# Substitution coefficients of the delta rule: fifteen shuffles within VectorE in place of a way through memory

## The chip, the cores and the metric

One Trainium2 chip, one core. The metric is the device time of one execution in microseconds (us). TensorE (PE) multiplies matrices, VectorE (DVE) and ScalarE (ACT) work on 128 partitions of elements, GpSimd (POOL) on few things here, and SyncE (SP) issues the DMA transfers. Each engine runs its own queue in order; semaphores join them.

## What is computed

A trunk of two layers over 256 positions and a width of 1024, in float32. A layer is a half-step SwiGLU network, a mixer, and a second such network. The mixer projects its input into three branches and their gates: A (sparse attention with an indexer that picks 64 keys per query), B (attention with forget gates) and C (gated DeltaNet). The change lies in C:

```python
def chunked_gated_delta_rule(q, k, v, g, beta):
    ...
    a_mat = jnp.where(strict, jnp.einsum('nbhid,nbhjd->nbhij', kb, kc) * decay, 0.0)
    m = a_mat + jnp.eye(cs, dtype=jnp.float32)
    rhs = jnp.concatenate([vc * bc[..., None], kb * jnp.exp(gc)[..., None]], axis=-1)
    sol = lax.linalg.triangular_solve(m, rhs, left_side=True, lower=True, unit_diagonal=True)
    ...
    y_c = rms_norm(o_c, delta_norm) * jax.nn.silu(c_z.reshape(b, s, C_HEADS, C_HEAD_DIM))
```

followed by `merged = gates[0] * y_a + gates[1] * y_b + gates[2] * y_c`, each y times a branch matrix of its own, and an output projection.

## The kernel before

All weights are streamed: SP issues `raw` tiles of 128 x 2 x 512 (line 121), ACT copies each to a rounded `hi`, DVE subtracts for the rest `lo` (lines 135 and 136), and PE multiplies with both. A weight unit has a number; in layer 0 the mixer has the units 48 to 127: 80 to 83 are `bv`, 84 to 91 the gates of branch A, 92 to 99 those of B, 100 to 103 branch A's matrix, 104 to 111 the gates of C, 112 to 115 branch B's matrix, 116 to 119 branch C's, 120 to 127 the output's. Three `hi` and `lo` are held at a time, so a `hi` waits until PE is through with the unit three before it.

The branches are generators (`branch_a`, `branch_b`, `branch_c`), which the class Emit steps along between the large matmuls by a plan of its own (`tick`, line 178): a step is due when the time that the plan gives to its engines has gone by, and no step is written while the planned DVE or ACT is over 6 us ahead of PE (`LIM`). `finish` (line 185) writes what is left of a branch before its matrix is used. A scheduler then orders the written instructions on each engine; the large tiles of one kind (`k4`, 20 of them) are handed out in the order of writing.

Branch C computes 8 triangular systems of 128 x 128 (two halves of the positions, four heads) by inverting their 16 x 16 diagonal blocks on DVE and merging the blocks upward on PE. `nT` holds the transposed matrix; `nd` its diagonal blocks, `cp16` (line 629) these packed to 128 x 128: partition 16k + i has, for each of the 8 systems, row i of block k. The substitution (lines 669 to 673) is, for m = 0 to 14, one product `ztmp<-nb,zc` and one difference `zc<-zc,ztmp`. Its coefficients `nb` must hold row m of a block in all 16 partitions of this block; they come through memory: `dr<-cp16` (line 632) writes 128 x 128 to DRAM, two transfers `nb<-dr` (line 634) read them back 16 times repeated, all three on SP's queue.

From `zc` come Z (the block inverse) and X, its transpose (lines 678 to 682). Then on PE, with a copy or a sum on ACT or DVE behind each: `lw` (blocks of 16 to 32), `lv` twice (32 to 64), `xz` (a transpose), `lv` twice (64 to 128), `vh` (the solve), `st` (state), `wv`, `ks`, `qs`, `vh` and `wv` for the second half of the positions, and `yc`. The last matmuls of the mixer's middle, `pbr` with `ych`, need them all.

Other names: `qs<-tq` and `ix` belong to branch A's queries and index scores, `score` and MAX/MATCH_REPLACE to its choice of keys, `lg` are logits in PSUM, `L` logits in SBUF and then softmax, `mx` their maximum, `pT`/`PT` transposed softmax, `pv`/`yh`/`yl` its product with the values, `bqk` and `bv` branch B's inputs, `gate` the copy of a gate's matmul out of PSUM.

Of the kernel before, what the change touches and what calls it, by code (L numbers as in the profile page):

```python
# [9 lines left out]
F32 = mybir.dt.float32  # L10
# [6 lines left out]
P = 128  # L17
# [177 lines left out]
def trunk_kernel(ctx: ExitStack, tc: tile.TileContext, x, consts, par, rows, bgate, fnorm,  # L195
                 wf1i, wf1o, wf2i, wf2o, wmx, wms, wbr, wmo, out, phases=None):
    nc = tc.nc
# [3 lines left out]
    rawp = ctx.enter_context(tc.tile_pool(name="rawp", bufs=NR))  # L201
    hlp = ctx.enter_context(tc.tile_pool(name="hlp", bufs=NH))
    wk = ctx.enter_context(tc.tile_pool(name="wk", bufs=2))
    dp = ctx.enter_context(tc.tile_pool(name="dp", bufs=2, space=bass.MemoryType.DRAM))
    ps = ctx.enter_context(tc.tile_pool(name="ps", bufs=4, space=bass.MemoryType.PSUM))
    pa = ctx.enter_context(tc.tile_pool(name="pa", bufs=2, space=bass.MemoryType.PSUM))
    pc = ctx.enter_context(tc.tile_pool(name="pc", bufs=2, space=bass.MemoryType.PSUM))
# [19 lines left out]
    V, S, G = E.V, E.S, E.G  # L227
# [11 lines left out]
    for u in range(4):  # L239
# [6 lines left out]
                                   ap=[[0, P], [N_ROW, DEPTH], [1, N_ROW]]))  # L246
# [12 lines left out]
    def k4(name, dt=F32):  # L259
        return wk.tile([P, 1024], dt, name=name, tag="k4", bufs=K4)  # L260
# [20 lines left out]
    def v3(t, a):  # L281
        return t.rearrange("p (a b) -> p a b", a=a)
# [210 lines left out]
    def tiny(name, n, bufs=2):  # L493
        return wk.tile([P, n], F32, name=name, tag="t_" + name, bufs=bufs)
# [80 lines left out]
    def branch_c(l, qkv, gd, hh, hl, need):  # L575
# [48 lines left out]
        nd, nb, zc = k4("nd"), [k4("nb") for _ in range(2)], tiny("zc", P, 1)  # L624
# [3 lines left out]
        cp16 = tiny("cp16", P, 1)  # L628
        V.tensor_reduce(v3(cp16, 8), nd.rearrange("p (q k r) -> p q r k", q=8, k=8), axis=AX.X, op=OP.add)
        V.tensor_copy(v3(zc, 8), cst[:, None, C_E16:C_E16 + 16].to_broadcast([P, 8, 16]))  # L630
        dr = dp.tile([P, P], F32, name="dr", tag="dr")
        nc.sync.dma_start(dr, cp16)
        for i in range(2):
            nc.sync.dma_start(nb[i], bass.AP(tensor=dr.tensor, offset=dr.offset + i * 1024,
                                               ap=[[2048, 8], [0, 16], [1, 1024]]))
        yield
        rk = tiny("rk", 8)
        G.tensor_tensor(out=rk, in0=ssk, in1=phalf, op=OP.pow)
        kdf = tiny("kdf", 4)
# [28 lines left out]
        tmp = tiny("ztmp", P, 1)  # L668
        for m in range(15):
            k = 15 - m  # L670
            V.tensor_tensor(out=v3(tmp, 8)[:, :, :k], in0=nb[m // 8].rearrange("p (m q r) -> p m q r", m=8, q=8)[:, m % 8, :, m + 1:],
                            in1=zv[:, :, m:m + 1].to_broadcast([P, 8, k]), op=OP.mult)
            V.tensor_tensor(out=zv[:, :, m + 1:], in0=zv[:, :, m + 1:], in1=v3(tmp, 8)[:, :, :k], op=OP.subtract)
            if m % 4 == 3:
                yield
# [325 lines left out]
    def mixer(pi, st):  # L1001
# [40 lines left out]
        with tc.high_priority(offset=EOFF):  # L1042
            for tb in range(2):
# [3 lines left out]
                S.activation(th, z, AF.Tanh, scale=0.5)  # L1047
                V.scalar_tensor_tensor(z, th, 1.0, z, op0=OP.add, op1=OP.mult)
        tcc = E.add(branch_c(l, qkv, gd, hh, hl, need), -1, CP)
        bqk = []  # L1050
        for i in range(2):
# [167 lines left out]
```

## Time and profile before

| | |
|---|---|
| runs | 1130.22 us median of 3 (1129.42 to 1130.91) |
| profiled execution | 1133.0 us, span 1131.2 us |
| PE busy | 1108.3 us, 98% |
| DVE busy | 842.2 us, 74% |
| ACT busy | 652.2 us, 58% |
| POOL busy | 198.0 us, 18% |

A busy PE is not PE at its peak, as matmuls overlap and their ends are modelled. What a change can win or lose is read from the places where PE stands, and from the granted clock of TensorE. The two mixers lie at 143 to 440 us and 700 to 1000 us; the second repeats the first.

### The profile page before, as it was taken

To read this page: it belongs to the slowest core of one execution; us is meant where nothing else is said; L and a number is where in the kernel's file an instruction comes from. 1 tells how busy PE (TensorE), PEld (TensorE's weight loads), DVE (VectorE), ACT (ScalarE), POOL (GpSimd) and SP (SyncE) were. 2 spreads that over 40 slices of the span, in tenths; PEclk is the share of its full clock that TensorE was granted. 3 is DMA by queue.
4 is the path that set the end of the run, shared out by engine and by line. 5 is a ranking of instruction groups with operands and counts; after the bars stand their busy time and mean duration, and the time that the engine had idled before them with its cause. 6 is when DMAs were issued, how large, how long until landed. Compare 5 with 4: busy or idle time off the path is not lost.

```text
span 1131.2 us, 17844 instructions
## 1 busy us (share of the span) xinstructions
PE 1108.3 (98%) x6765; PEld 954.2 (84%) x6765; DVE 842.2 (74%) x1373; ACT 652.2 (58%) x1136; POOL 198.0 (18%) x172
## 2 busy tenths in 40 slices
PE   9999999998999999999999999999999999999997
PEld 7888898987778878888888889979877788888886
DVE  7776689879746677876678767888796658787753
ACT  6655455644758645655465645564647685556543
POOL 4322022100000203322032311040000003033210
PEclk9999999999999999999999999999999999999999
DMA  8665655555434354666556555555554344556652
GB/s 285 205 186 189 190 178 184 165 146 167 149 113 144 128 179 154 213 195 188 187 171 202 186 193 182 177 169 168 152 177 150 104 130 147 169 171 200 187 191 91
DMA packets 56375, 194.07 MB, mean 172 GB/s; under 512 B 6240, under 2 KB 8672, under 8 KB 56288
## 3 DMA queue, kind: packets, MB, share of 16 engines
q1 hardware_dynamic: 55856, 192.32, 53.2%
q8 instruction: 53, 0.87, 0.3%
q10 hardware_dynamic: 432, 0.60, 0.1%
q14 instruction: 34, 0.28, 0.1%
HBM read 191.72 MB, written 1.18 MB: 171 GB/s over the span
## 4 chain that ended last, share of the span: by engine, by line
PE 91%; DVE 4%; DMA 2%; issue 1%; POOL 1%; ACT 1%; POOLq 0%; DVEq 0%; ACTq 0%
PE pw L148 48%; PE pt L148 25%; PE pbr L148 6%; PE po L148 4%; DMA nb<-dr 2%; DVE lo L86 1%; PE lg L148 1%; PE pv L148 1%; PE pT L152 1%; PE lv L148 1%; PE lw L148 1%; DVE score L86 1%; PE gq L148 1%; DVE ztmp L86 0%; POOL rp L86 0%
## 5 line engine op out<-in xcount | busy, mean ns | idle before, releaser
L86 DVE TENSOR_TENSOR lo<-raw,hi 128x1024 fp32r<-128x1024 f32 (+2 forms) x353 | 451.2, 1280 | 178.8 <-ACT hi L86 178.2
L86 ACT ACTIVATE hi<-raw 128x1024 fp32r<-128x1024 f32 (+2 forms) x353 | 372.6, 1057 | 353.9 <-PE pw L148 155.7
L148 PE MATMUL pw<-xt,hi 128*128 128x512 f32 x1024 | 349.0, 396 | 0.8 <-ACT hi L86 0.8
L148 PE MATMUL pw<-xt,lo 128*128 128x256 f32 x1024 | 263.8, 280 | 0.0
L148 PEld LDWEIGHTS pw<-xt,hi 128*128 128x128 f32 x1024 | 189.3, 189 | 37.7 <-ACT hi L86 1.7
L148 PE MATMUL pt<-hi,xt 128*128 128x512 f32 (+1 forms) x640 | 206.5, 398 | 4.7 <-DVE gate L86 4.7
L148 PEld LDWEIGHTS pw<-xt,lo 128*128 128x128 f32 x1024 | 193.0, 189 | 9.0 <-DVE lo L86 0.7
L148 PEld LDWEIGHTS pt<-hi,xt 128*128 128x128 f32 x640 | 120.5, 191 | 28.7 <-issue 5.8
L148 PE MATMUL pw<-ht,hi 128*128 128x512 f32 x384 | 132.2, 394 | 0.0
L148 PE MATMUL pt<-lo,xt 128*128 128x512 f32 (+1 forms) x320 | 127.9, 400 | 1.7 <-DVE lo L86 1.7
L148 PE MATMUL pt<-xt,hi 128*128 128x256 f32 x640 | 118.1, 285 | 0.0
L148 PE MATMUL pw<-ht,lo 128*128 128x256 f32 x384 | 103.4, 279 | 0.0
L148 PEld LDWEIGHTS pt<-xt,hi 128*128 128x128 f32 x640 | 99.6, 191 | 0.2
L148 PE MATMUL pt<-xt,lo 128*128 128x256 f32 x320 | 89.7, 284 | 0.0
L148 PEld LDWEIGHTS pw<-ht,hi 128*128 128x128 f32 x384 | 71.4, 188 | 15.2
L86 POOL TENSOR_TENSOR hr<-hg,rbc 128x512 f32<-128x512 f32 x32 | 42.3, 1323 | 213.8 <-DVE hg L86 204.5
L148 PEld LDWEIGHTS pw<-ht,lo 128*128 128x128 f32 x384 | 72.4, 188 | 1.5
L148 PEld LDWEIGHTS pt<-lo,xt 128*128 128x128 f32 x320 | 61.0, 191 | 14.2 <-DVE lo L86 2.6
L86 POOL TENSOR_TENSOR hg<-hr,rbc 128x512 f32<-128x512 f32 x32 | 66.9, 2090 | 2.5
L86 POOL TENSOR_TENSOR ssum<-ssum,sq 128x512 f32<-128x512 f32 x18 | 28.6, 1588 | 199.3 <-ACT sq L86 199.3
L148 PEld LDWEIGHTS pt<-xt,lo 128*128 128x128 f32 x320 | 60.8, 191 | 0.0
L86 POOL TENSOR_TENSOR so<-so,mhalf 128x8 f32<-128x8 f32 x2 | 3.3, 1642 | 284.9 <-DVE so L86 284.9
(254 smaller groups left out, 1498.6 us busy)
## 6 DMA issues: line engine op xcount, KB each, us to landing
raw<-in_wmx SPq DMA_DIRECT2D x112, 512.0 KB, 3.7
raw<-in_wf2i SPq DMA_DIRECT2D x64, 512.0 KB, 3.8
raw<-in_wf1i SPq DMA_DIRECT2D x63, 512.0 KB, 4.2
raw<-in_wf1o SPq DMA_DIRECT2D x32, 512.0 KB, 4.2
raw<-in_wf2o SPq DMA_DIRECT2D x32, 512.0 KB, 4.2
raw<-in_wbr SPq DMA_DIRECT2D x24, 512.0 KB, 3.3
raw<-in_wmo SPq DMA_DIRECT2D x16, 512.0 KB, 4.1
raw<-in_wms SPq DMA_DIRECT2D x8, 468.0 KB, 3.8
```

The lines of the kernel that those rows point to most:

```text
L86: return f(*args, **kw)
L148: self.nc.tensor.matmul(out, lhsT, rhs, start=start, stop=stop, skip_group_check=True)
L152: self.nc.tensor.transpose(out, in_, ident)
```

## The change

The DRAM tile and the three transfers go. In their place DVE writes `nb` itself: for each m one `stream_shuffle`, which gives every partition of a group of 32 the content of one partition out of this group, by a list of 32 places. The list for m sends partition m to partitions 0 to 15 and partition 16 + m to 16 to 31. Only the columns that the substitution reads are written, 8 x (15 - m). Where one `yield` stood behind the transfers, there are now three, one after each five shuffles. Nothing else is changed in the text.

```diff
-    dp = ctx.enter_context(tc.tile_pool(name="dp", bufs=2, space=bass.MemoryType.DRAM))
...
-        dr = dp.tile([P, P], F32, name="dr", tag="dr")
-        nc.sync.dma_start(dr, cp16)
-        for i in range(2):
-            nc.sync.dma_start(nb[i], bass.AP(tensor=dr.tensor, offset=dr.offset + i * 1024,
-                                               ap=[[2048, 8], [0, 16], [1, 1024]]))
-        yield
+
+        nbv = [t.rearrange("p (m q r) -> p m q r", m=8, q=8) for t in nb]
+        for m in range(15):
+            V.stream_shuffle(nbv[m // 8][:, m % 8, :, m + 1:], v3(cp16, 8)[:, :, m + 1:],
+                             [16 * (i // 16) + m for i in range(32)])
+            if m % 5 == 4:
+                yield
...
-            V.tensor_tensor(out=v3(tmp, 8)[:, :, :k], in0=nb[m // 8].rearrange("p (m q r) -> p m q r", m=8, q=8)[:, m % 8, :, m + 1:],
+            V.tensor_tensor(out=v3(tmp, 8)[:, :, :k], in0=nbv[m // 8][:, m % 8, :, m + 1:],
```

The plan and the scheduler order the mixer anew from there on. Outside the mixers the order is the same; in each mixer it differs from the first shuffle to the matmuls with `ych`. DVE before, where the coefficients are waited for (`ztmp` waits for `nb`):

```order
L86 TENSOR_REDUCE cp16_2544<-nd_2538 128x128
L86 TENSOR_TENSOR lo81_2706<-raw81_2512,hi81_2705 128x1024
L86 TENSOR_SCALAR aq_2653<-aq_2653 128x8
L86 TENSOR_TENSOR bqk_2557<-pt_2295,rbc8_1619 128x512
L86 TENSOR_TENSOR bqk_2557<-pt_2296,rbc8_1619 128x512
L86 TENSOR_TENSOR lo82_2762<-raw82_2566,hi82_2761 128x1024
L86 TENSOR_TENSOR qs_2239<-tq_2589,qs_2239 64x4x128
L86 TENSOR_TENSOR qs_2239<-tq_2598,qs_2239 64x4x128
L86 TENSOR_TENSOR ztmp_2803<-nb_2539,zc_2541 128x8x15
L86 TENSOR_TENSOR qs_2240<-tq_2589,qs_2240 64x4x128
```

DVE now, the same place:

```order
L86 TENSOR_TENSOR lo81_2696<-raw81_2510,hi81_2695 128x1024
L86 STREAM_SHUFFLE nb_2537<-cp16_2542 128x8x15
L86 TENSOR_TENSOR bqk_2556<-pt_2293,rbc8_1617 128x512
L86 TENSOR_TENSOR bqk_2556<-pt_2294,rbc8_1617 128x512
L86 STREAM_SHUFFLE nb_2537<-cp16_2542 128x8x14
...
L86 STREAM_SHUFFLE nb_2537<-cp16_2542 128x8x8
L86 TENSOR_TENSOR qs_2237<-tq_2588,qs_2237 64x4x128
L86 TENSOR_TENSOR qs_2237<-tq_2597,qs_2237 64x4x128
L86 TENSOR_TENSOR ztmp_2878<-nb_2537,zc_2539 128x8x15
L86 TENSOR_TENSOR lo82_2736<-raw82_2565,hi82_2735 128x1024
L86 TENSOR_SCALAR aq_2754<-aq_2754 128x8
```

Eight shuffles stand ahead of `qs`; `lo82` has moved behind them and behind the first `ztmp`. The other seven follow 12 places later. On ACT, the two copies `bv<-pt` have moved from behind `hi93` to behind `hi85`.

Z, the result of the substitution, on DVE before, right behind the last `zc`:

```order
L86 TENSOR_TENSOR zc_2541<-zc_2541,ztmp_2803 128x8
L86 MAX m8_2970<-score_2620 128x8
L86 TENSOR_TENSOR Z_2897<-zc_2541,cst_109 128x512 x2
L86 MATCH_REPLACE score_2620<-m8_2970,score_2620 128x256
L86 STREAM_TRANSPOSE X_2898<-Z_2897 128x512 x2
```

DVE now, where Z stands (`lo104` belongs to the gates of C, `L_3128` is the first softmax of branch B):

```order
L86 TENSOR_TENSOR lo104_3865<-raw104_3785,hi104_3864 128x1024
L86 SCALAR_TENSOR_TENSOR gate_3817<-pt_3743,rstd_1583,bg_3741 128x512
L86 SCALAR_TENSOR_TENSOR gate_3817<-pt_3744,rstd_1583,bg_3741 128x512
L86 TENSOR_TENSOR L_3128<-lg_3131,cst_107 128x512
L86 TENSOR_TENSOR Z_3178<-zc_2539,cst_107 128x512
L86 TENSOR_TENSOR L_3128<-lg_3132,cst_107 128x512
L86 TENSOR_TENSOR Z_3178<-zc_2539,cst_107 128x512
L86 SCALAR_TENSOR_TENSOR mrg_2890<-gate_3617,pbr_3862 128x512
L86 STREAM_TRANSPOSE X_3179<-Z_3178 128x512
```

The last `zc` stands 36 places ahead of this Z; before it was two. PE before, around the second half of the first `lv` (unit 99 are gates of B, 100 is A's matrix):

```order
L148 MATMUL lv_3320<-Z_2897,T1_2899 32x32 x8
L148 MATMUL lv_3330<-Z_2897,T1_2899 32x32 x8
L148 MATMUL pt_3735<-hi98_3736,xt_1074 128x512
...
L152 MATMUL pT_3108<-cst_109,L_3062 128x128 x4
L152 MATMUL xz_3349<-cst_109,Z_2897 64x64 x8
L148 MATMUL pbr_3813<-hi100_3772,yh_3104 128x512
L148 MATMUL pbr_3813<-lo100_3773,yh_3104 128x512
L152 MATMUL pT_3115<-cst_109,L_3062 128x128 x4
L148 MATMUL lv_3393<-X_2898,nT_2382 64x64 x8
```

PE now, behind the last matmul of the gates of C (unit 111):

```order
L148 MATMUL pt_3986<-hi111_4005,xt_1073 128x512
L148 MATMUL lv_3375<-Z_3178,T1_3180 32x32 x8
L148 MATMUL lv_3385<-Z_3178,T1_3180 32x32 x8
L152 MATMUL xz_3398<-cst_107,Z_3178 64x64 x8
L148 MATMUL lv_3411<-X_3179,nT_2380 64x64 x8
L148 MATMUL lv_3430<-Z_3178,T1_3180 64x64 x8
L148 MATMUL vh_3458<-rv_2813,Z_3178 128x128 x4
L148 MATMUL st_3492<-T1_3180,kd_2814 128x128 x4
L148 MATMUL wv_3498<-T1_3180,wT_2381 128x128 x4
L148 MATMUL ks_3516<-St_3457,fmk_1765 128x128 x4
L148 MATMUL qs_3527<-St_3457,fmq_1621 128x128 x4
```

Where softmax and weight matmuls lay between the steps, there is nothing now; behind `qs` follow `pv` of branch B, the second `vh`, a `pT` and the first `pbr` with branch B's `yh`.

## Rows read from the trace of the kernel before

**Rows 1.** The page, the chain that ended last, by engine.
```profile
PE 91%; DVE 4%; DMA 2%; issue 1%; POOL 1%; ACT 1%; POOLq 0%; DVEq 0%; ACTq 0%
```
**Rows 2.** Waits of PE, whole run: us in total, times, longest.
```profile
PE pt L148 <- DVE gate L86: 4.7, 2, 2.4
PE ix L148 <- DVE qs L86: 2.5, 4, 1.1
...
PE pt L148 <- DVE lo L86: 1.7, 2, 0.9
```
**Rows 3.** Windows: length, busy us (instructions) by engine, PEclk, DMA share, GB/s.
```profile
251.50:256.50 5.00, 2.66 (x14) 1.62 (x14) 4.35 (x11) 2.68 (x9) 0.00 (x0) 1.00 0.48 128
272.17:274.51 2.34, 0.00 (x0) 0.03 (x1) 2.34 (x6) 1.17 (x2) 0.00 (x0) 1.00 0.66 210
276.24:279.65 3.41, 3.41 (x10) 2.63 (x10) 3.41 (x11) 0.00 (x0) 0.00 (x0) 0.53 0.52 193
285.00:343.00 58.00, 58.00 (x469) 45.49 (x466) 37.38 (x52) 39.22 (x89) 0.00 (x0) 1.00 0.42 137
289.06:289.63 0.57, 0.57 (x8) 0.57 (x5) 0.57 (x2) 0.57 (x2) 0.00 (x0) 1.00 0.79 57
343.00:393.00 50.00, 50.00 (x302) 40.92 (x301) 31.78 (x47) 38.81 (x101) 4.29 (x4) 1.00 0.38 125
```
**Rows 4.** The tile nb, who waited for it; window ahead of the first gate.
```profile
  DMA nb<-dr: 9.3, 2
...
241.23:273.62 32.39, 28.60 (x148) 23.45 (x146) 26.42 (x69) 17.17 (x35) 0.00 (x0) 1.00 0.57 167
```
**Rows 5.** Timeline of DVE: start us, us, line, operation, [idle before <-releaser].
```profile
251.92 0.28 DVE L86 TENSOR_TENSOR ztmp<-nb,zc 128x120 f32<-128x120 f32 x1 [4.84 <-DMA nb<-dr]
252.24 0.69 DVE L86 TENSOR_TENSOR qs<-tq,qs 64x512 fp32r<-64x512 f32 x1
...
254.00 0.28 DVE L86 TENSOR_TENSOR ztmp<-nb,zc 128x112 f32<-128x112 f32 x1
254.31 0.28 DVE L86 TENSOR_TENSOR zc<-zc,ztmp 128x112 f32<-128x112 f32 x1
...
255.11 1.22 DVE L86 TENSOR_TENSOR lo<-raw,hi 128x1024 fp32r<-128x1024 f32 x1
256.25 0.25 DVE L86 TENSOR_TENSOR ztmp<-nb,zc 128x96 f32<-128x96 f32 x1
...
267.99 0.09 DVE L86 MATCH_VALUE_LOAD score<-m,score 128x8 f32 x1
268.07 0.41 DVE L86 MATCH_REPLACE8 score<-m,score 128x256 f32<-128x256 f32 x1
...
273.62 1.40 DVE L86 SCALAR_TENSOR_TENSOR gate<-pt,rstd,bg 128x512 f32<-128x512 f32 x2
...
277.34 1.27 DVE L86 TENSOR_TENSOR Z<-zc,cst 128x512 f32<-128x512 f32 x2
```
**Rows 6.** Timeline of PE, ACT and DVE at steps of branch C and beside them.
```profile
253.08 0.36 PE L148 MATMUL ix<-akh,iqs 128*128 128x256 f32 x1 [1.14 <-DVE qs L86]
...
324.70 1.14 PE L148 MATMUL lv<-X,nT 64*64 64x64 f32 x16
325.77 1.08 PE L148 MATMUL pv<-PT,sm 128*64 128x256 f32 x8
...
325.88 0.59 ACT L86 ACTIVATE T<-lv 64x512 f32<-64x512 f32 x1 [0.47 <-PE lv L148]
...
339.71 1.28 DVE L86 TENSOR_TENSOR L<-lg,cst 128x512 f32<-128x512 f32 x2
```
**Rows 7.** Timeline of PE and ACT at ks and qs.
```profile
359.80 1.16 PE L148 MATMUL ks<-St,fmk 128*128 128x128 f32 x8
360.80 1.06 PE L148 MATMUL qs<-St,fmq 128*128 128x128 f32 x8
...
361.00 1.15 ACT L86 ACTIVATE eks<-ks,eg 128x128 f32<-128x128 f32 x4 [1.37 <-PE ks L148]
```

## Prediction

> **What bounds the kernel now.** I read the chain that ended last first: it is TensorE (PE) for 91% [rows 1]. So a change elsewhere pays only where PE stands still. The list of waits, cut to PE, names three places that belong to this change: PE waited 4.7 us for VectorE's (DVE's) `gate`, 2.5 us for its `qs` and 1.7 us for its `lo`, two layers together, 8.9 us in all [rows 2]. [...]
>
> Why DVE is late: `ztmp` at 251.92 had to wait 4.84 us for the landing of `nb<-dr` [rows 5], and twice that in both layers, 9.3 us [rows 4]. Behind it in DVE's queue stand the last two `qs`, then `lo` and at 273.62 the `gate` [rows 5]. The third `qs` ends at 252.93 and PE's `ix` starts at 253.08 [rows 5, 6]. From 241.23 to 273.62 DVE worked 26.42 of 32.39 us [rows 4].
>
> **Part 1, the transfers go.** With the wait go the PE waits that it passed on: at most 8.9 us, and the half-clock stretch, 3.41 us in a layer in which half the work is lost, 1.7 us, or 3.4 in both layers (the second repeats the first). Ceiling: 12.3 us. The six transfers that leave SP's queue (2 `dr`, 4 `nb`) were waited for by `ztmp` alone; nobody else gains.
>
> **Part 2, fifteen shuffles a layer come to DVE.** They write 8 x (15 + ... + 1) = 960 elements per partition. No row of before shows a shuffle, so I bound it. From below: `lo` starts at 255.11 and the next instruction 1.14 us later, 1024 elements at 1.07 us and 0.07 us beside them [rows 5]; 960 elements and 15 starts give 1.0 + 1.05 = 2.1 us. From above: `ztmp` at 254.00 with 120 elements holds its successor, which needs its result, for 0.31 us, 0.185 us beside the elements [rows 5]; 15 of these, and 0.08 us each for a load ahead, as MATCH_REPLACE8 has one (267.99 to 268.07) [rows 5], give 1.0 + 2.8 + 1.2 = 5.0 us. Nothing excludes either end. I take 3.2 us: the lower price with the load, since each shuffle brings a list of 32 places of its own and none needs the one ahead of it.
> [...]
>
> What is queued behind them: eight stand ahead of the four `qs`, the others between `bqk` and the first `score`. What else the order moves across the first `gate`: behind it go `lo89` (1.14), a MAX, a MATCH_REPLACE and three `ztmp`/`zc` pairs (some 1.4); ahead come two `L` and an `mx` of 1024 elements (some 2.4). So DVE has 26.4 + 3.2 - 0.2 = 29.4 us of work ahead of `gate`, and with 0.5 for short holds it reaches it near 271.1 in place of 273.62. PE, freed of 4.7 us of waits in this layer and with eight `lg` now ahead (four took 0.57 us [rows 3], so 1.2), comes to the matmuls of the weights 88 near 274.51 - 4.7 + 1.2 = 271.0. They no longer wait for `gate`, as ScalarE (ACT) now empties the banks of `bv` early, but for `lo88` and `lo89`, just ahead of `gate` and just behind it: I allow a PE wait of 0.5 us a layer. DVE has no slack over these 30 us, so each further microsecond of shuffle is one of PE's: none at 2.1 us, 2.4 at 5.0. Both layers: 1.0 (0 to 4.8).
>
> **Part 3, the substitution's product comes much later.** This the diff doesn't tell and the order does. Before, `Z<-zc` stands right behind the last `zc` and ran at 277.34 [rows 5]. Now it stands 36 places behind the last `zc`, directly behind the first `L` of branch B, which before ran at 339.71 [rows 6]: 62 us later. Everything that follows from Z (`lw`, `lv`, `xz`, `vh`, `st`, `wv`, `ks`, `qs`) follows. Before, these small steps lay among large matmuls, and PE had no gap from 285 to 393 [rows 3]. Now the last large matmul of the gate 2 weights stands ahead of the second round of `lv`, and from there PE's queue holds `xz`, `lv`, `lv`, `vh`, `st` one behind another, each of which reads what ACT has just copied from the one ahead. What a bare step costs: `lv` at 324.70 gives way to the next matmul at 325.77, and ACT's copy starts 0.11 us after that and lasts 0.59 [rows 6]; the way back is the 0.15 us from `qs` to `ix`. That is 0.85 us of standing PE. Four steps (`lv`, `lv`, `vh`, `st`) are 3.4 us, and `xz`, partly covered, 0.6. `ks` is covered by `wv`.
> Then the first matmuls with `yh` of branch B: ACT's copy of `yh` now stands behind four `eks`, two `PT`, two `junk` and four `X`: 1.1 + 1.1 + 0.7 + 1.1 + 0.6 = 4.6 us after `ks` [rows 6, 7] (`PT` and `yh` priced like the copy behind `lv`, a `junk` like a quarter of `eks` with its reading out); PE has `qs`, `pv`, `vh` and a `pT` to do in that time, 36 records, at eight in 1.0 us from `ks` to `qs` [rows 7] and a little quicker within a kind: an estimate of 3.2 us, as the records of `pv` and `pT` are short. It stands still for some 1.4 us, and 0.4 more at `vh` (for `rv`) and `wv`. Sum 5.8 us a layer, 11.6 in both. Bounds: half of it (5.8), if the copies overlap with what precedes them better than bare; and 15, if ACT comes to the first copy late (it gets there only some 0.4 us ahead of PE, with `hi113` and four `L` in front).
>
> **Sum.** -12.3 + 1.0 + 11.6 = +0.3 us on the profiled execution of 1133.0 us, 1.8 of it outside the span. The median of the runs is 1130.2, so I forecast 1130.5. What the shuffles win in the first half of the mixer, the late chain gives back in the second.
>
> **Rivals.** *The chain finds cover (faster).* Part 3 costs only its lower bound: 1130.2 - 12.3 + 1.0 + 5.8 = 1124.7. For it: PE had no gap in all of the second half before [rows 3], so there is a reserve in the other engines; against it: the bare steps are bound to each other by data, and no engine's speed shortens a copy of 0.59 us.
> *The clock falls in the bare chain (slower).* From the first bare step to `ks` PE stands for some 4 of 9 us. After 2.34 us in one piece the clock fell; in the 5 us behind 251.5, with PE busy for 2.66, it stayed at 1.00 [rows 3]. The bare chain is like the second in its share and longer. If the clock falls once a layer it costs what it cost before, 1.7 us, so 3.4: 1133.9; twice, 1137.3.
> *The shuffle is dear (slower).* At 5.0 us a layer the PE wait of part 2 is 4.8 and not 1.0: 1134.3. It decides from 4.2 us a layer, 0.28 a shuffle, on: there part 2 costs 3.0 and the time is 1132.5. For it: a shuffle that must wait for its load, or the load for the shuffle ahead, costs like a dependent instruction; against it: the load of MATCH_REPLACE8 costs 0.08 us.
> That the change doesn't do what it says is excluded by the order: no transfer of `nb` or `dr` is left.
>
> **How the numbers follow.** A measurement of this kernel can tell some 0.2%, 2.3 us, from no change: below 1128.0 is faster, above 1132.5 slower. The forecast gets 0.42, and as its terms are uncertain by some 2 us, 0.07 of that falls below and 0.05 above. Cover: 0.27, all faster. Clock: 0.20, 0.17 of it slower. Dear shuffle: 0.11, 0.10 of it slower. Faster 0.34, same 0.34, slower 0.32. The range goes from 1123, below the covered chain, to 1137.5, the clock falling twice; about 0.1 on either side is left out.
>
> **What would show it.** Part 1: no DVE wait on a DMA near 250, and PE's waits for `qs` gone. Part 2: the shuffles' group adds to 3 us a layer; above 4 the dear case. Part 1 and 2 together: no row of granted clock near 0.5 behind `gate`. Part 3: PE waits for ACT's `T`, `Z`, `X` and `St`, each near 0.85 us, and one near 1.4 for `yh`, between 355 and 375; if they are missing or half as long, the cover case holds. If PE waits at `lo88` by over 2 us, DVE's queue is longer than I add it up. A time outside the range would mean an effect beyond the mixer, which no row lets me expect: outside it the two orders are the same.

## The result: slower by 0.7%

The changed kernel takes 1138.3 us (1137.4 to 1140.1), the kernel before 1130.6 in the runs beside it; the ratio is 1.0067, 95% interval 1.0046 to 1.0087. That is 0.8 us above the range of the forecast. The profiled execution took 1137.5 us, 1.8 of it outside its span of 1135.7.

The chain that ended last still lies on PE; the 2% of the transfers are gone [rows 1]:

```profile
PE 91%; DVE 4%; ACT 2%; issue 1%; POOL 1%; DMA 0%; SPq 0%; POOLq 0%; DVEq 0%; ACTq 0%
```

The waits of PE over the whole run (us in total, times, longest), against [rows 2]:

```profile
PE mt L152 <- DVE mrg L86: 2.6, 2, 1.3
...
PE pv L148 <- ACT PT L86: 1.6, 2, 0.8
PE st L148 <- ACT T L86: 1.5, 2, 0.7
PE lv L148 <- ACT T L86: 1.4, 2, 0.7
PE lv L148 <- ACT X L86: 1.4, 2, 0.7
PE vh L148 <- ACT Z L86: 1.4, 2, 0.7
...
PE xz L152 <- ACT Z L86: 1.0, 2, 0.5
...
PE pt L148 <- DVE bqk L86: 0.6, 2, 0.3
PE pbr L148 <- DVE gate L86: 0.4, 2, 0.2
```

and a row of before that grew:

```profile
PE mt L152 <- DVE mrg L86: 1.4, 2, 0.7
```

The three waits of before (4.7, 2.5 and 1.7 us) are gone. In their place stand six on ACT that before had not: five for steps of the substitution's chain, and `pv` of branch B, which stands right behind it, for `PT`. They add to 8.3 us in both layers. `mt` waits 1.2 us more than before and a few short waits are new, so all the waits listed for PE add to 18.3 us, before to 16.2: by waits alone the changed kernel would lose 2 us. The rest is in the windows (length, busy us of PE, PEld, DVE, ACT, POOL, then PEclk); the first three are windows of [rows 3], the others the chain:

```profile
251.50:256.50 5.00, 5.00 (x29) 4.37 (x29) 4.92 (x28) 4.74 (x13) 0.00 (x0) 1.00 0.58 198
276.24:279.65 3.41, 3.41 (x17) 2.83 (x16) 3.07 (x9) 1.15 (x2) 0.00 (x0) 1.00 0.85 292
285.00:343.00 58.00, 58.00 (x351) 45.32 (x351) 40.45 (x55) 39.42 (x91) 0.00 (x0) 1.00 0.49 159
...
357.26:360.00 2.74, 1.73 (x41) 1.46 (x40) 1.23 (x1) 2.25 (x4) 0.00 (x0) 1.00 0.57 191
360.00:373.65 13.65, 11.35 (x65) 10.68 (x66) 0.00 (x0) 3.52 (x8) 0.00 (x0) 0.50 0.12 40
373.65:378.00 4.35, 3.53 (x37) 3.06 (x36) 0.69 (x1) 4.17 (x16) 0.00 (x0) 1.00 0.00 0
```

The first half of the mixer became what the change is for: PE is busy without a gap behind 251.5, and the clock behind `gate` stays full. But from 360.00 to 373.65 the granted clock is 0.50, for 13.65 us, four times as long as the 3.41 us of before [rows 3]. PE is busy for 11.35 us of them; if all that work went at half the pace, half of it would be lost, 5.7 us. The second layer has a stretch of 13.65 us too. The timeline of PE there shows both losses (start us, us, then what, with idle time before it and its releaser):

```profile
357.26 1.09 PE L148 MATMUL lv<-Z,T 32*32 32x32 f32 x32
358.88 0.64 PE L152 MATMUL xz<-cst,Z 64*64 64x64 f32 x8 [0.52 <-ACT Z L86]
360.19 1.96 PE L148 MATMUL lv<-X,nT 64*64 64x64 f32 x16 [0.68 <-ACT X L86]
362.84 1.97 PE L148 MATMUL lv<-Z,T 64*64 64x64 f32 x16 [0.68 <-ACT T L86]
365.48 2.08 PE L148 MATMUL vh<-rv,Z 128*128 128x128 f32 x8 [0.68 <-ACT Z L86]
368.30 2.08 PE L148 MATMUL st<-T,kd 128*128 128x128 f32 x8 [0.74 <-ACT T L86]
...
371.88 1.91 PE L148 MATMUL ks<-St,fmk 128*128 128x128 f32 x8
373.58 1.10 PE L148 MATMUL qs<-St,fmq 128*128 128x128 f32 x8
375.51 1.09 PE L148 MATMUL pv<-PT,bv 128*64 128x128 f32 x16 [0.82 <-ACT PT L86]
```

The waits of one layer are 0.52 + 3 x 0.68 + 0.74 + 0.82 = 4.1 us. And a `ks` that took 1.16 us [rows 7] takes 1.91, an `lv` of 64 1.96 in place of 1.14 [rows 6].

On VectorE the shuffles and what follows from them:

```profile
253.46 0.01 DVE L86 LOAD_MASK_SELECT nb<-cp  x1
253.46 0.22 DVE L86 STREAM_SHUFFLE nb<-cp 128x48 f32<-128x48 f32 x1
253.59 0.01 DVE L86 LOAD_MASK_SELECT nb<-cp  x1
253.59 0.22 DVE L86 STREAM_SHUFFLE nb<-cp 128x40 f32<-128x40 f32 x1
253.70 0.02 DVE L86 LOAD_MASK_SELECT nb<-cp  x1
253.70 0.20 DVE L86 STREAM_SHUFFLE nb<-cp 128x32 f32<-128x32 f32 x1
...
268.69 0.75 DVE L86 SCALAR_TENSOR_TENSOR gate<-pt,rstd,bg 128x512 f32<-128x512 f32 x1
...
321.49 0.68 DVE L86 TENSOR_TENSOR L<-lg,cst 128x512 f32<-128x512 f32 x1
322.08 0.68 DVE L86 TENSOR_TENSOR Z<-zc,cst 128x512 f32<-128x512 f32 x1
```

Here the next shuffle starts 0.11 to 0.13 us after the one ahead of it, though each is listed with 0.20 to 0.22: they overlap. The first `gate` is at 268.69, five us earlier than before [rows 5]. `Z` runs at 322.08, 45 us later than before [rows 5], directly behind the first `L` of branch B.

### The profile page after: what moved, and what is told of

Its sections match the earlier page's. It is cut to its first block, busy times and chain, and to the rows that moved or that the text cites. A ratio compares the mean times of both kernels' runs of the same rounds, so it can differ in the third digit from the quotient of the medians.

```text
span 1135.7 us, 17901 instructions
## 1 busy us (share of the span) xinstructions
PE 1110.7 (98%) x6765; PEld 959.7 (85%) x6765; DVE 848.5 (75%) x1433; ACT 650.5 (57%) x1136; POOL 198.2 (17%) x172
## 4 chain that ended last, share of the span: by engine, by line
PE 91%; DVE 4%; ACT 2%; issue 1%; POOL 1%; DMA 0%; SPq 0%; POOLq 0%; DVEq 0%; ACTq 0%
PE pw L148 47%; PE pt L148 28%; PE po L148 4%; PE pbr L148 3%; DVE lo L86 2%; PE lg L148 2%; PE pv L148 1%; PE pT L152 1%; PE lv L148 1%; PE lw L148 1%; ACT hi L86 1%; PE gq L148 1%; DVE mtmp L86 1%; PE vh L148 1%; PE wv L148 0%
## 5 line engine op out<-in xcount | busy, mean ns | idle before, releaser
L148 PE MATMUL pt<-hi,xt 128*128 128x512 f32 (+1 forms) x640 | 202.8, 392 | 0.6 <-DVE bqk L86 0.6
```

Of the source, the lines that this page charges most:

```text
L148: self.nc.tensor.matmul(out, lhsT, rhs, start=start, stop=stop, skip_group_check=True)
```

## The experiments

Theory: the change itself gains some 10 us, and the late chain, which its new writing order makes, costs more: the waits and the fallen clock. The rival is that the shuffles, on a VectorE without slack, cost what is lost. Medians of runs on the same chip beside the kernel before (1131.2 to 1132.1 there).

**The shuffles without the planner's account** (`uncharged`).

```diff
-            V.stream_shuffle(nbv[m // 8][:, m % 8, :, m + 1:], ...
-            if m % 5 == 4:
-                yield
+            nc.vector.stream_shuffle(nbv[m // 8][:, m % 8, :, m + 1:], ...
+        yield
```

> The same fifteen shuffles a layer, but the planner is not told of them and gives way once instead of three times, so that it writes the rest of the mixer almost as in the kernel before: the substitution's steps again stand between large matmuls. Theory (late chain): the whole loss of the change comes from the chain of substitution steps that stands bare behind the gate C matmuls (8 us of waits and twice 13.65 us at half clock in the profile); without it the gain of the first half stays, 8.9 us of waits and 1.7 us of half clock a layer: 1118 to 1121 us, no stretch at half clock ahead of the last 10 us. Rival (the shuffles themselves): VectorE has no slack from 240 to 275 us, and the shuffles' 3.9 us a layer are paid whatever the order: 1126 to 1138 us.

1127.2 us, ratio 0.9965 (0.9953 to 0.9978). With the same shuffles the loss turns into a gain; no PE wait for a step of the chain is left and no half clock in it. But the time is 6 us above the theory's band and lies in the rival's (1126 to 1138), so this run alone does not refute the rival; `reuse` below does, with the same shuffles 7.5 us faster. Of these 7.5 us the profile here shows 1.5 us of waits for `zc`, 1.3 for `bqk` (0.6 there) and 3.41 us at half clock at the end of the second mixer, at most 1.7 us of loss. What else: from the mixer's first `pt` to its first `mt` the large matmuls (`pt` and `pbr`) and the small ones take turns 113 to 115 times a layer, against 87 in `reuse`, and by the starts in the trace the first large matmul of 512 columns behind a turn mostly holds its successor for 0.31 to 0.34 us, where it is 0.23 otherwise. PE comes back to large matmuls 27 times more in both layers; at 0.09 us that would be 2.4 of the 3.6 us left. That this is the remainder is argued, not shown.

**The transfers with the planner's account** (`dma_planned`): the kernel before, and in place of its one `yield`:

```diff
+        for m in range(15):
+            cost = V.fixed + V.per * 8 * (15 - m)
+            V.t = max(V.t, E.t) + cost
+            E.chain = max(V.t, E.chain + cost + (0.0 if E.last is V else 0.15))
+            E.last = V
+            E.fin = max(E.fin, E.chain)
+            if m % 5 == 4:
+                yield
```

> The kernel before with its transfers, no shuffle in it; only the planner is told of fifteen VectorE instructions and gives way three times, as in the changed kernel. In the order the steps lv, lv, xz, lv, lv, vh, st, wv, ks, qs stand one behind another, as in the changed kernel. Theory (late chain): the loss comes without any shuffle: between 1138 (the wait for the transfer hidden by the new order) and 1150 us (1130.6 plus 8.3 of waits and 11 of half clock), and a stretch at half clock of 10 us or more a layer. Rival (the shuffles themselves): within 2 us of the kernel before, 1130.6.

1148.1 us, ratio 1.0152 (1.0137 to 1.0167): the loss, with no shuffle in the kernel. Its PE waits have the chain's five rows to the digit, `pv` with more, and three others in the first half of the mixer, those of the kernel before with `junk` in the place of `gate`:

```profile
PE pt L148 <- ACT junk L86: 4.2, 2, 2.1
...
PE pv L148 <- ACT PT L86: 2.3, 2, 1.6
PE ix L148 <- DVE qs L86: 2.3, 4, 0.9
...
PE vh L148 <- ACT Z L86: 1.4, 2, 0.7
PE lv L148 <- ACT X L86: 1.4, 2, 0.7
...
PE pt L148 <- DVE lo L86: 1.1, 1, 1.1
```

The stretches at half clock in the chain are 10.24 and 13.65 us; one of 3.41 stands in the first half of each mixer, as before, and a third at the end of the second. So the order alone costs 16.5 us, and in nearly this order (about a tenth of the mixer's matmuls stand elsewhere) the shuffles gain 1148.1 - 1138.3 = 9.8.

**One break in place of three** (`one_yield`), the planner told of the shuffles.

```diff
-            if m % 5 == 4:
-                yield
+        yield
```

> The changed kernel with one break behind the fifteen shuffles in place of three, the planner told of them. In the order lv(32) and xz lie between large matmuls again, the second lv(64), vh, st, wv, ks, qs stand bare as in the changed kernel. Theory (a bare step costs 0.7 us, and the clock falls when PE has stood still in several of them one after another): three or four waits a layer in place of six, 1125 us if the clock holds, 1131 to 1135 if it falls there too, the stretch then shorter than 13.65 us. Rival (the shuffles themselves): as the changed kernel, 1137 to 1140.

1129.2 us, ratio 0.9983 (0.9972 to 0.9994). `vh`, `st` and `pv` stand bare (0.7, 0.7, 0.8 us of wait a layer), and in the profiled execution the clock holds in the chain: with these three bare steps it did not fall there. The median lies between the two numbers of the theory; a wait for `bqk` of 1.2 us a layer, 0.3 in the changed kernel, and 3.41 us at half clock at the end of the second mixer stand against the lower one.

**Z, X and T1 in dead buffers** (`reuse`): the changed kernel in all else.

```diff
-        Z, X, T1 = k4("Z"), k4("X"), k4("T1")
+        Z, X, T1 = nb[0], nb[1], nd
```

> The changed kernel in all, planner told and three breaks; only Z, X and T1 take the buffers of nb and nd, which are dead by then, in place of new ones from the pool that hands out its twenty buffers in the order in which the code is written. In the order the steps stand between large matmuls again, save lv, vh, st, which stand between them in blocks. Theory (late chain, and the place in the pool's row is what makes it late): 1118 to 1124 us, no half clock there. Rival (the planner's writing order alone makes it late): Z still late, 1136 to 1139. Rival (the shuffles themselves): 1130 or more.

1119.7 us, ratio 0.9900 (0.9885 to 0.9916): faster than both kernels. Its PE waits, all of them:

```profile
PE mt L152 <- DVE mrg L86: 2.7, 2, 1.3
PE ti L152 <- POOL sm L86: 2.2, 2, 1.1
PE pw L148 <- DVE mp L86: 1.7, 2, 0.9
PE spin L237 <- DVE phalf L86: 1.2, 1, 1.2
PE pw L148 <- ACT hi L86: 1.1, 2, 0.7
PE pt L148 <- DVE bqk L86: 0.6, 2, 0.3
```

And its window of the chain:

```profile
285.00:393.00 108.00, 108.00 (x779) 87.19 (x778) 71.47 (x99) 69.84 (x163) 7.79 (x5) 1.00 0.43 135
```

One line takes 18.6 us from the changed kernel. No row of the substitution is left, and nothing stands still from 285 to 393.

**More buffers, and a row of their own** (`k4_21`, `ownrow19`): is a buffer short, or does the pool hand them out in the order in which the code is written, `Z` behind `L`?

```diff
-K4 = 20
+K4 = 21
```

> The changed kernel with 21 buffers in the pool of Z, X and T1 in place of 20. PE's and VectorE's order come out as in the changed kernel, Z directly behind the first L of branch B. Theory (what holds Z back is its place in the row in which the pool hands out buffers, behind L of branch B, and not that a buffer is short): as the changed kernel, 1136 to 1140 us, half clock again for some 13 us a layer. Rival (a shortage of buffers): 1118 to 1125.

1138.8 us, ratio 1.0061 (1.0046 to 1.0076), in the profiled execution 10.24 us at half clock in the chain of each layer and 3.41 at the end of each mixer. PE's order is that of the changed kernel matmul for matmul, so the same order gave 13.65 us in one execution and 10.24 in another.

```diff
-K4 = 20
+K4 = 19
-        Z, X, T1 = k4("Z"), k4("X"), k4("T1")
+        Z, X = [wk.tile([P, 1024], F32, name=s, tag="zx", bufs=2) for s in "ZX"]
+        T1 = nd
```

> The changed kernel with Z and X in two buffers of their own, a row of their own (the pool is left with 19, T1 takes the buffer of nd); the planner's account and the three breaks are those of the changed kernel. PE's order comes out like that of the kernel with the buffers of nb and nd. Theory (the row): 1118 to 1121 us. Rival (taking dead buffers is what helps, as it leaves more to the others): 1125 or more.

1119.4 us, ratio 0.9892 (0.9875 to 0.9909). Twenty-one buffers in one row change nothing; nineteen and two in a row apart cure it. That speaks for the row. It is not the last word on a shortage, as in `ownrow19` three tiles a layer no longer draw on the row, and more than 21 buffers in it were not tried.

**Three breaks without the account** (`y3unch`), to tell which of the two things that the planner sees moves `Z`.

```diff
-            V.stream_shuffle(nbv[m // 8][:, m % 8, :, m + 1:], ...
+            nc.vector.stream_shuffle(nbv[m // 8][:, m % 8, :, m + 1:], ...
```

> The changed kernel with its three breaks, the planner not told of the fifteen shuffles; Z, X and T1 from the pool. In the order Z is early again and the chain stands between large matmuls. Theory (of the two things that the planner sees it is the account of VectorE's time that moves the writing order, the breaks are harmless): 1117 to 1124 us, no half clock in the chain. Rival (each break gives way to other work, so the chain comes late): 1130 to 1139.

1126.3 us, ratio 0.9948 (0.9931 to 0.9965), no half clock in the chain. It missed the theory's band by 2 us, but is well below the rival's. `Z` runs at 273.3 us here, in `uncharged` at 273.8, in `one_yield` at 309.4 and in the changed kernel at 322.1: the account of VectorE's time moves it, and the three breaks move it further only together with the account. The large and small matmuls take turns 105 to 111 times a layer, and like `uncharged` it stands some 7 us above `reuse`.

**Work in PE's gaps** (`hold`): how much of the chain's price is the clock? Two matmuls on zeros ahead of `xz`, both `lv` of 64, `vh` and `st`, into the bank that the step then overwrites.

```diff
+        def hold(pt, n=2):
+            o = pt if len(pt.shape) == 2 else pt.rearrange("p a b c -> p (a b c)")
+            for _ in range(n):
+                nc.tensor.matmul(o, idle[:, :P], idle, start=True, stop=True, ...)
...
                     pt = pc.tile([P, 512], F32, name="lv", tag="s")
+                    if b == 64:
+                        hold(pt)
...
```

> The changed kernel; ahead of each of the five bare steps xz, lv, lv, vh and st PE now does two matmuls of 128x512 on zeros into the bank that the step itself then overwrites, in the 0.5 to 0.7 us in which it stood still. They compute nothing and no step has less to wait for. Theory (two halves: some 4.4 us a layer is the waiting, the larger half, 13.65 us at half clock with PE busy for 11.35 of them, is the clock that fell because PE stood still again and again): the stretch at half clock is gone or much shorter, 5 us a layer come back: 1126 to 1130 us. Rival (the waits alone count, the clock costs nothing since PE waits for copies anyway): no gain, 1138 to 1141, the clock back or not. Rival (the clock falls because of the small tiles of lv, not because of the gaps): still half clock from 360 on, 1138 to 1143.

1132.2 us, ratio 1.0012 (0.9991 to 1.0033): 6.1 us come back from work that computes nothing. The chain in the timeline of PE:

```profile
359.39 0.38 PE L679 MATMUL xz<-idle 128*128 128x512 bf16 x1 [0.52 <-ACT Z L86]
359.92 0.63 PE L152 MATMUL xz<-cst,Z 64*64 64x64 f32 x8
360.48 0.60 PE L679 MATMUL lv<-idle 128*128 128x512 bf16 x2
361.23 1.14 PE L148 MATMUL lv<-X,nT 64*64 64x64 f32 x16
...
363.05 1.14 PE L148 MATMUL lv<-Z,T 64*64 64x64 f32 x16
...
364.88 1.16 PE L148 MATMUL vh<-rv,Z 128*128 128x128 f32 x8
...
366.78 1.16 PE L148 MATMUL st<-T,kd 128*128 128x128 f32 x8 [0.53 <-ACT T L86]
...
369.62 1.06 PE L148 MATMUL qs<-St,fmq 128*128 128x128 f32 x8
```

And its window from the last `lv` of 32 to `pv`:

```profile
357.78:371.50 13.72, 11.27 (x121) 8.79 (x122) 1.66 (x2) 7.37 (x17) 0.00 (x0) 1.00 0.24 78
```

The clock is 1.00 and `lv` takes 1.14 us again. From the last `lv` of 32 to `pv` it is 13.7 us, in the changed kernel 357.26 to 375.51, 18.3: 4.5 us a layer come back, beside 4.1 of waits that no filling shortens. Step by step the clock had cost a little more: the two `lv` 0.8 each, `vh` 0.9, and from the start of `st` to that of `qs` 5.28 us against 2.84, in all 5.0 us a layer. The filling itself takes about the difference, as its first matmuls start only when the wait for `Z` is over and `xz` follows 0.53 us behind them. The small tiles of `lv`, the same here, do not make the clock fall by themselves: it is 1.00 over them. The median lies 2 us above the theory's band; in the profiled execution 3.41 us at half clock came later in the first layer, from 405.4. In eight of the ten runs the mean granted clock was 0.994 to 0.997 and the time 1130.0 to 1133.9 us; in two it was 0.987 and 0.985, as in the changed kernel, and the time 1138.4 and 1140.1. The filling holds the clock mostly, not always.

**Every shuffle twice** (`twice`), on top of `reuse`.

```diff
             V.stream_shuffle(nbv[m // 8][:, m % 8, :, m + 1:], v3(cp16, 8)[:, :, m + 1:], ...
+            nc.vector.stream_shuffle(nbv[m // 8][:, m % 8, :, m + 1:], v3(cp16, 8)[:, :, m + 1:], ...
```

> The kernel with Z, X and T1 in the buffers of nb and nd, with every shuffle issued twice (the second writes the same again): fifteen more shuffles a layer on VectorE, which the planner is not told of. From start to start a shuffle cost 0.09 us (8 elements) to 0.20 (96 to 120), fifteen 2.1 us. Theory (the shuffles are nearly free: they fill gaps of VectorE and the path goes through PE): within 2 us of the kernel with single shuffles, 1118 to 1122 us. Rival (VectorE, 33.21 busy in 33.50 us from 241.5 on, has no slack there, each shuffle is paid in full): 2.1 us a layer more, 1123.5 to 1126.

1121.8 us, ratio 0.9912 (0.9891 to 0.9933). Thirty more shuffles in both layers, 4.2 us of VectorE by the starts, moved the median by 2.1 us, half of that time, and the intervals overlap; the theory's band (1118 to 1122) holds it. The order moved with them, so this is no clean price; it makes it likely that the single shuffles cost no more than a few tenths of a per cent.

**The transfers with the dead buffers** (`reuse_before`): does that line alone make a kernel faster?

```diff
-        Z, X, T1 = k4("Z"), k4("X"), k4("T1")
+        Z, X, T1 = nb[0], nb[1], nd
```

> The kernel before with its transfers, with Z, X and T1 in the buffers of nb and nd; no shuffle. Theory (the gain of 11 us of the shuffled kernel with these buffers is that of the transfers gone; before had no late chain to cure): 1128 to 1132 us, PE's waits for gate, qs and lo and the half clock behind gate as before. Rival (the buffers themselves are the gain, whatever moves the coefficients): 1119 to 1124.

1129.9 us, ratio 0.9998 (0.9982 to 1.0014): no. The waits for `qs` and `lo` stay:

```profile
PE ix L148 <- DVE qs L86: 2.4, 4, 1.2
...
PE pt L148 <- DVE lo L86: 1.7, 2, 0.9
```

But not all came as expected: the 4.7 us of `gate` and the half clock behind it are gone, with the transfers still there, and 3.41 us at half clock stand at the end of the second mixer instead. Against `reuse` the shuffles gain 10.2 us, though the planner is not told the same in the two; the next kernel is the closer one to compare.

**The dead buffers without the account** (`reuse_unch`): `uncharged` and `reuse` together.

```diff
-            V.stream_shuffle(nbv[m // 8][:, m % 8, :, m + 1:], ...
-            if m % 5 == 4:
-                yield
+            nc.vector.stream_shuffle(nbv[m // 8][:, m % 8, :, m + 1:], ...
+        yield
...
-        Z, X, T1 = k4("Z"), k4("X"), k4("T1")
+        Z, X, T1 = nb[0], nb[1], nd
```

> The shuffles with Z, X and T1 in the buffers of nb and nd, the planner not told of the shuffles and one break behind them in place of three. In the order the steps of the chain stand between large matmuls as with the planner told. Theory (the place in the pool's row decides, not the planner's account): within 3 us of the kernel with these buffers and the planner told, 1117 to 1122 us. Rival (the planner's account matters as much, since it costs 7 us where Z keeps its own buffer): 1124 to 1128.

1119.9 us, ratio 0.9897 (0.9872 to 0.9922). Once `Z` does not stand in the row, the planner's account no longer matters. Against `reuse_before`, where the planner sees as little, the shuffles gain 10.0 us.

## Why the forecast was wrong, step by step

*What bounds the kernel, and part 1.* Right in its number. The waits for `gate`, `qs` and `lo` and the half clock behind `gate` went with the transfers. The shuffles in place of the transfers gain 9.8 us in nearly the changed order (`dma_planned`) and 10.0 with the dead buffers (`reuse_before` to `reuse_unch`); parts 1 and 2 had -12.3 + 1.0 = -11.3. That the gain consists of the rows that I had listed is not shown: `reuse_before` has neither the waits for `gate` nor the half clock behind it and still takes 10.0 us more, of which its waits (13.6 us in all against 10.8) and its one stretch at half clock account for less than half.

*Part 2.* Right in size, and the shuffle is cheaper than I took it: a layer's fifteen add to 2.1 us from start to start, which is the lower bound, not 3.2. The loads exist, and are short:

```profile
L86 DVE LOAD_MASK_SELECT nb<-cp x30: 5/14/21, 241.6 to 813.7; - x30
```

One stands ahead of each shuffle, thirty in two layers, at a median of 14 ns. No row of before showed a load of a shuffle: the forecast assumed one and took it at 0.08 us from that of MATCH_REPLACE8, which was the nearest row and six times too dear. VectorE came to the first `gate` at 268.69, not 271.1, and PE had no wait at `lo88`; it waits 0.3 us a layer for `bqk`, which now stands behind the first shuffle. That is 0.6 us for the 1.0 of the forecast, at another place than I had it, so the nearness is luck. (The wait of `pbr` for `gate`, 0.2 us a layer, is in `dma_planned` too, where no shuffle is.)

*Part 3, the place.* Right: `Z` directly behind the first `L` of branch B, 45 us later than before and not 62, as this `L` too came earlier, and behind the gate C matmuls the bare `xz`, `lv`, `lv`, `vh`, `st`, each waiting for ACT. The single waits came out at 0.52 to 0.74 us and not 0.85, and PE did not wait for `yh` but 0.82 us for `PT`: 4.1 us a layer in place of 5.8.

*Part 3, the price: the step that failed.* The term of 11.6 us counted the chain at full clock and left the clock to a rival with a chance of 0.20. `dma_planned` shows the late chain at +16.5 us, `reuse` is 18.6 below the changed kernel; 8.3 of it are waits and the greater part is the clock, some 10 us, 5.0 a layer by the steps of `hold` (4.5 that came back there, 5.7 as the upper end by the window). 8.3 and 10 add to 18.3. The rival itself had the mechanism and the wrong size: it took the length of a fall from the one row of before, 3.41 us [rows 3], so 1.7 us of loss. Here the bare steps go on while the clock is down, it stays at 0.50 for 13.65 us, and PE is busy for 11.35 of them. That its double fall gave 1137.3, one us from the measured 1138.3, is two errors that meet: it had 6.8 us of clock where some 10 were lost, and 11.6 us of waits where 8.3 came.

*The reason against the rival* was a window of 5 us in which PE was busy for 2.66 and the clock stayed [rows 3]. That one row did not carry what I hung on it.

*Sum.* With the measured terms: -10 for the change proper, +18.3 for the late chain, +8.3; measured +7.8.

*A time outside the range would mean an effect beyond the mixer*: wrong. From the first `pt` of a mixer to its first `mt` the changed kernel takes 263.6 and 263.2 us, before 261.1 and 261.0, and all the rest of the two profiled executions agrees to 0.2 us (that of before lies 2.8 us above its median, so the two differ by less than the medians do). The loss came from inside, from the term whose upper bound of 15 I had not let the clock into.

## What to carry to other kernels

When a change hands a planner new costs, compare the order of what comes after it first, and look whether a step that moved is held by a row of buffers in writing order: here one line, three buffers that were dead anyway, turned a loss of 0.7% into a gain of 1.0%. Price a chain of small dependent steps that stands bare on TensorE twice, once for the waits and once with the clock at the 0.50 of these traces over the whole stretch, and give the second a large chance: with six such waits a layer the clock fell in each of the three profiles here, for 10.24 to 13.65 us (the changed kernel, `dma_planned`, `k4_21`), with three it held in the chain at 1.00 (`one_yield`). To tell the two apart, put matmuls on zeros into the gaps.

## What was not expected of the hardware

The granted clock fell to 0.50 without any long stand: ahead of 360.00 PE had a gap of 0.52 us and the start of one of 0.68, and was busy for 1.73 of the 2.74 us; in the kernel before it had stood still for 2.34 us in one piece [rows 3]. And it stayed down with PE busy for 11.35 of 13.65 us. Yet it held at 2.66 busy of 5.00 us [rows 3], and in `one_yield` with three such gaps of 0.7 to 0.8 us; what decides between these rows stays open. A shuffle with its load cost VectorE 0.09 us at 8 elements and 0.19 at 120 from start to start.
